# A transformer block on one Trainium2 core: half a column group of the feed-forward input projection moved to the seven-product scheme, and its weight blocks prepared beside the output projection

## The chip, the core and the metric

The kernel runs on one core of a Trainium2 chip. A core has a matrix engine (TensorE, PE in the profile, with PEld for its weight loads), a vector engine (VectorE, DVE), a scalar engine (ScalarE, ACT), a general engine (GpSimd, POOL) and a queue engine (SyncE, SP), which here only issues transfers. Each engine works through its own list of instructions in order and waits at semaphores for the others. Matrix products are accumulated in PSUM, which has eight banks, b0 to b7; everything else lies in SBUF. The metric is the device time of one execution, in microseconds (us).

## What is computed

One decoder block for 512 tokens and a width of 1024. What matters here is its end: the output projection with its residual, the second normalization, and the input projection of a SwiGLU feed-forward network with 2816 hidden columns.

```python
x = x + gate1 * (merged @ w_out)
h2 = rms_norm(x, norm2_g) * (1.0 + scale2) + shift2
f_g, f_u = jnp.split(h2 @ w_ffn_in, 2, axis=-1)
x = x + gate2 * ((jax.nn.silu(f_g) * f_u) @ w_ffn_out)
```

## The kernel before

**Precision.** A product is made of three matmuls (`mm3`, lines 52 to 55): each operand is split into a rounded part `hi` and the rest `lo`, and hi·hi, hi·lo and lo·hi are summed. A weight block therefore costs one ACT copy (to `hi`) and one DVE subtraction (to `lo`) before PE can use it.

**Weights.** They come in blocks of 512 KB. For most of the kernel they are a `stream`: `ensure(n)` issues the transfers ahead (line 92, on SP) into a ring of three buffers, tag `raw` (`RAWB = 3`), and prepares the chunks up to n (`prep`, ACT at L110 and DVE at L114). A transfer is issued when the preparation of the chunk that had the buffer before has been done.

**Output projection** (the loop over `half`). Tokens go in two halves of 256. For each half, eight chunks of `w_out` (n_ = 0 to 7) give two column halves: for the second token half, n_ = 0 to 3 make the first column half and n_ = 4 to 7 the second. Each n_ is 12 matmuls of 128x512 into `po`. When a column half is complete, `resid` adds it to x (two DVE operations, L1108 and L1109, and a square on ACT, L1110, for each of two token tiles). When both are there, `row_rstd` (L1113, L1114) and `norm2_x` (L1130 on ACT, L1132 on DVE) give the normalized rows `xn`.

**Transposes** (`norm2_T`). `xn` of one token half is transposed on PE (L1154) by pairs of 128 columns: pair k2 = 0 to 3 has four transposes into one bank and holds kt = 2·k2 and 2·k2 + 1. From there each kt is evacuated three times: ACT writes `hi` (L1161), DVE (or, for every fourth kt, ACT: L1164) writes the full value `h2f` (L1166), and DVE subtracts to get `lo` (L1167). For token half 0 this is done behind n_ = 2 of token half 1 of the output projection, with pairs 0 to 3 in banks 4 to 7; for token half 1 within group 0, below.

**Group 0 of the feed-forward input** (`pf`). The 2816 gate columns and the 2816 up columns are worked off in groups of 256. Group 0 is done directly: four chunks `WF[0]` to `WF[3]` (gate kh = 0 and 1, up kh = 0 and 1, where kh is the half of the 1024 inputs), each 24 matmuls of 128x256 for each token half. Order: token half 0 with gate kh 0, gate kh 1, up kh 0, then the transposes of token half 1, up kh 1; then token half 1 with all four. `EV` evacuates the sums (L1225 on ACT, L1231 on DVE).

**The direct half of group 1** (`pb`). The gate columns of group 1 are done directly too, with two more stream chunks.

**Seven products.** From the up columns of group 1 on (q = -1 to 17; q even is the gate half, q odd the up half of group 2 + q // 2) a block of 1024 inputs x 256 columns times 512 tokens is cut into 2 x 2 halves on both sides and done with seven half-size products instead of eight (a Winograd form of Strassen's scheme). On the token side the differences of `h2f` are made once (`t_diff`, L1242 to L1245) and split into `TB[1]` to `TB[4]` (`t_split`, L307 and L308). On the weight side `s_issue(q)` fetches two blocks, `ra` (kh 0) and `rb` (kh 1), and `s_prep(q)` gives four pairs of steps, an ACT part a and a DVE part d:

- a0 and d0: `hi` of A11, then on DVE A21 + A22 (L1295, the first that reads both blocks), `lo` of A11 (L1296) and a difference (L1297);
- a1 and d1: `hi` and `lo` of rb (L1301, L1304), then rb less that difference (L1305);
- a2 and d2: `hi` and `lo` of ra (L1309, L1312); a3 and d3: of the new rb (L1316, L1319).

The steps of block q + 1 are laid between the products of block q, so on ACT and DVE they stand in one line with what the products themselves need: copies of sums (`R`, L1537 and L1550; `ps`, L1544 and L1557), which PE waits for before it adds to the bank further on, silu or multiplication at the end (L1527, L1533, L1525, L1531) and two sums (L1562, L1565). One block has 84 matmuls of 128x256, twelve for each product, in the order A, C (S1), C (S2), B (A12), D (S3), D (S4), B (A22).

The order of every engine's list is the order of the program text; nothing is rescheduled.

Of the kernel before, what the change touches and what calls it, by code (L numbers as in the profile page):

```python
# [9 lines left out]
F32 = mybir.dt.float32  # L10
# [7 lines left out]
D = 1024  # L18
# [10 lines left out]
def block_kernel(ctx: ExitStack, tc: tile.TileContext, x, positions, w_ada, b_ada, w_in,  # L29
# [230 lines left out]
    for n_, (h, k0) in enumerate(((0, 0), (1, 0), (0, 2), (1, 2), (0, 4), (0, 6), (1, 4), (1, 6))):  # L260
        W_O.append((h, add_w(w_o, [k0, k0 + 1], 512 * h, 512, V, (None, None, None, "E2", "E0", "E1", "E3", "E4")[n_])))
    mg = mod_sec(5)
    W_F = []
    for g in range(2):
        wh = ["E5", "E6", "E0", "E1"] if g == 0 else None
        W_F.append([group(w_ffn_in, 256 * g, where=wh)])
        if g == 0:
            W_F[0].append(group(w_ffn_in, DFF, where=wh))
    st["limit"] = len(stream)

    KZ, KC = (list(range(12, 16)), list(range(16, 20))), list(range(12)) + [20, 21]
# [859 lines left out]
            else:  # L1131
                V.tensor_scalar(xn[tk], xt[tk], r2[:, tk:tk + 1], None, op0=OP.mult)  # L1132

    def norm2_T(half, kts):
        if half == 0:
            for kh in range(2):
                t = ffn[0].tile([128, 4, 256], F32, name="h2f", tag=f"F{kh}", bufs=1)
                for j in range(4):
                    h2f[kh * 4 + j, 0] = t[:, j]
                h2f["t", kh, 0] = [t[:, 0:2], t[:, 2:4]]  # L1140
        else:
            for kh in range(2):
                h2f["t", kh, 1] = []
                for q in range(2):
                    t = base.tile([128, 2, 256], F32, name="h2f", tag=f"S1_{kh * 2 + q}", bufs=1)
                    h2f["t", kh, 1].append(t)
                    for j in range(2):
                        h2f[kh * 4 + q * 2 + j, 1] = t[:, j]
        for k2 in kts:
            p = bank(4 + k2, "x2T")  # L1150
            for k in range(2):
                kt = k2 * 2 + k
                for e in range(2):
                    T.transpose(p[:, k * 256 + e * 128:k * 256 + (e + 1) * 128],  # L1154
                                xn[2 * half + e][:, kt * 128:(kt + 1) * 128], ident)
            for k in range(2):
                kt = k2 * 2 + k
                g, s = Gc[:, 1, kt:kt + 1], Gc[:, 1, 8 + kt:9 + kt]
                src = p[:, k * 256:(k + 1) * 256]
                hi, lo = (t[:, kt % 4] for t in HB[kt // 4, half])  # L1160
                A.activation(hi, src, AF.Identity, scale=g, bias=s)  # L1161
                hf = h2f[kt, half]
                if kt % 4 == 3:
                    A.activation(hf, src, AF.Identity, scale=g, bias=s)  # L1164
                else:
                    V.tensor_scalar(hf, src, g, s, op0=OP.mult, op1=OP.add)  # L1166
                V.tensor_sub(lo, hf, f(hi))  # L1167

    wch = {}
    WF0 = W_F[0][0] + W_F[0][1]  # L1170
# [76 lines left out]
    def t_split(n):  # L1247
# [7 lines left out]
    NQ = 18  # L1255
    sraw, sw = {}, {}

    def s_issue(q):
        if q >= NQ:
            return  # L1260
        c0 = (2 + q // 2) * 256 + (DFF if q % 2 else 0)
        sraw[q] = []
        for kh in range(2):
            if q % 2 and kh:
                t = ffn[0].tile([128, 4, 2, 128], F32, name="raw", tag="F0", bufs=1)
            else:
                t = base.tile([128, 4, 2, 128], F32, name="raw", tag="raw", bufs=RAWB)
            SY.dma_start(t.rearrange("p j a n -> p j (a n)"),
                         w_ffn_in[kh * 512:(kh + 1) * 512, c0:c0 + 256].rearrange("(j p) n -> p j n", p=128))
            sraw[q].append(t)  # L1270

    def s_pair(q, n):
        if q % 2 == 0:
            return (base.tile([128, 4, 2, 128], F32R, name="hi", tag="hi", bufs=3),
                    base.tile([128, 4, 2, 128], F32R, name="lo", tag="lo", bufs=3))
        if n < 2:
            t = ffn[0].tile([128, 2, 4, 2, 128], F32R, name="sx", tag=f"E{n}", bufs=1)
            return t[:, 0], t[:, 1]
        return tuple(base.tile([128, 4, 2, 128], F32R, name="sx", tag=f"S2_{2 + e}", bufs=1) for e in range(2))

    def s_prep(q):

        if q >= NQ:
            return z_first()
        ra, rb = sraw[q]
        d = sw[q] = {}
        A11, A21, A12, A22 = ra[:, :, 0], ra[:, :, 1], rb[:, :, 0], rb[:, :, 1]

        def a0():
            d["A"] = tuple(base.tile([128, 4, 128], F32R, name="sa", tag=f"S1_{4 + 2 * (q % 2) + e}", bufs=1)  # L1290
                           for e in range(2))
            A.activation(d["A"][0], A11, AF.Copy)

        def d0():
            V.tensor_add(A21, A21, A22)  # L1295
            V.tensor_sub(d["A"][1], A11, f(d["A"][0]))  # L1296
            V.tensor_sub(A11, A21, A11)  # L1297

        def a1():
            d["B"] = s_pair(q, 0)  # L1300
            A.activation(d["B"][0], rb, AF.Copy)  # L1301

        def d1():
            V.tensor_sub(d["B"][1], rb, f(d["B"][0]))  # L1304
            V.tensor_sub(rb, rb, A11[:, :, None, :].to_broadcast([128, 4, 2, 128]))  # L1305

        def a2():
            d["C"] = s_pair(q, 1)
            A.activation(d["C"][0], ra, AF.Copy)  # L1309

        def d2():
            V.tensor_sub(d["C"][1], ra, f(d["C"][0]))  # L1312

        def a3():
            d["D"] = s_pair(q, 2)
            A.activation(d["D"][0], rb, AF.Copy)  # L1316

        def d3():
            V.tensor_sub(d["D"][1], rb, f(d["D"][0]))  # L1319
        return [(a0, d0), (a1, d1), (a2, d2), (a3, d3)]  # L1320


    mgl = list(mg)
# [129 lines left out]
    for half in range(2):  # L1453
        o = slice(half * 256, (half + 1) * 256)
        for w in range(2):
            for ci, i in enumerate(W_F[0][w]):
                hi, lo = chunk[i]
                for j, kt in enumerate(stream[i]["kts"]):
                    for m in range(2):
                        cc = slice(m * 128, (m + 1) * 128)  # L1460
                        mm3(pf[w][m][:, o], (hi[:, j, cc], lo[:, j, cc]), tuple(t[:, j] for t in HB[ci, half]),
                            kt + half == 0, kt == 7, skip_group_check=True)
                if half == 0 and w == 1 and ci == 0:
                    norm2_T(1, range(4))
            if half == 0 and w == 1:
                t_diff()
                ensure(W_F[1][0][0])
            if half == 1:
                EV[w](0)(pf[w])
                ensure(W_F[1][0][1])  # L1470
                if w == 0:
                    t_split(1)
                    s_issue(-1)
                else:
                    t_split(2)
    pre = None
    pb = [bank(b, "pf1") for b in (5, 6)]
    for ci, i in enumerate(W_F[1][0]):
        hi, lo = get(i, 1)
        for j in range(4):  # L1480
            for m in range(2):
                cc = slice(m * 128, (m + 1) * 128)
                for th in range(2):
                    mm3(pb[m][:, th * 256:(th + 1) * 256], (hi[:, j, cc], lo[:, j, cc]),
                        tuple(t[:, j] for t in HB[ci, th]), ci + j + th == 0, ci == 1 and j == 3,
                        skip_group_check=True)
        if ci == 0:
            s_issue(0)
            pre = s_prep(-1)
        for a_, d_ in pre[2 * ci:2 * ci + 2]:  # L1490
            a_()
            d_()
            if d_ is pre[2][1]:
                t_split(3)
    f_evac(1)(pb)


    def sprod(o, wb, hb, start):
# [2 lines left out]
            mm3(o, (wh[:, j], wl[:, j]), (bh[:, j], bl[:, j]), start and j == 0, j == 3, skip_group_check=True)  # L1501

    left = []
    for q in range(-1, NQ):
        g, u = 2 + q // 2, q % 2
        d = sw[q]
        s_issue(q + 2)
# [36 lines left out]
        A.activation(ps[0], R[3], AF.Copy)  # L1544
# [242 lines left out]
```

## Time and profile before

| | |
|---|---|
| Time before, median of 3 runs | 840.51 us (840.35 to 841.24) |
| The profiled execution | 839.88 us, of which the span from the first to the last instruction is 838.0 us |
| DVE, ACT, POOL busy | 79%, 48%, 14% of the span |
| Transfers | 109.09 MB, mean 130 GB/s |
| Granted TensorE clock | 0.998 |

A row of the timeline gives the start, the duration, the engine, the line, the operation, "output <- input" by the program's names, the shape and how many were merged; in brackets stands how long the engine had been idle and what ended that. Matmuls are pipelined: what PE can do is read from the distance between starts, which is shorter than the duration of one. The windows give, for each engine, the busy time in a stretch, with the granted clock, the transfer share and GB/s at the end. A transfer's time to landing counts from its issue.

### The profile page before, as it was taken

The page shows a single profiled execution, that of the slowest core. Times are in us where ns is not written, and L with a number is a line of the kernel's source. Part 1 is how long each engine was busy: PE and PEld are TensorE (multiplying, and loading weights), DVE is VectorE, ACT ScalarE, POOL GpSimd, SP SyncE. Part 2 cuts the span into 40 slices and gives each one's busy share as a digit, 9 for nine tenths or more (in the row PEclk, how much of TensorE's full clock was granted, in tenths as well). Part 3 has the DMA queues.
Part 4 walks back from the last instruction along what each step waited for, and adds up shares of the span by engine and source line. Part 5 has one row for each costly group of instructions (what it writes and reads, how often), then busy time and mean ns, then how long its engine had stood idle before and what let it go on. Part 6 is the DMA issues. An engine that isn't in the chain of part 4 may idle for free.

```text
span 838.0 us, 12892 instructions
## 1 busy us (share of the span) xinstructions
PE 825.4 (98%) x5004; PEld 734.8 (88%) x5004; DVE 664.6 (79%) x1152; ACT 399.6 (48%) x696; POOL 118.2 (14%) x105
## 2 busy tenths in 40 slices
PE   7999999999999999999999999999999999999996
PEld 6888889988888888988888899999999999888885
DVE  7978799788899548887776568989998888985635
ACT  6664445332332227665434355655555555663322
POOL 2060022353344411002210000000000000000001
PEclk9999999999999999999999999999999999999999
DMA  9962362432346551037544032445543334142212
GB/s 299 311 190 72 95 200 78 127 90 86 109 145 200 189 163 51 26 102 248 174 142 165 1 126 76 127 153 156 172 149 102 101 101 150 53 149 101 78 51 100
DMA packets 95677, 109.09 MB, mean 130 GB/s; under 512 B 5617, under 2 KB 76273, under 8 KB 95617
## 3 DMA queue, kind: packets, MB, share of 16 engines
q1 hardware_dynamic: 92512, 101.37, 38.8%
q0 software_dynamic: 2384, 6.10, 2.0%
q8 instruction: 39, 0.64, 0.3%
q10 hardware_dynamic: 720, 0.82, 0.3%
q14 instruction: 22, 0.17, 0.1%
HBM read 105.90 MB, written 2.10 MB: 129 GB/s over the span
## 4 chain that ended last, share of the span: by engine, by line
PE 96%; DMA 1%; DVE 1%; issue 0%; SPq 0%; ACT 0%; POOLq 0%; POOL 0%; DVEq 0%
PE pb L53 9%; PE pb L55 9%; PE pb L54 9%; PE R L53 8%; PE R L54 8%; PE R L55 8%; PE pfo L55 4%; PE pfo L53 4%; PE pfo L54 4%; PE pav L54 2%; PE pav L53 2%; PE pav L55 2%; PE po L54 2%; PE pgb L53 2%; PE pgb L54 2%; PE pgb L55 2%
## 5 line engine op out<-in xcount | busy, mean ns | idle before, releaser
L110 ACT ACTIVATE hi<-raw 128x1024 fp32r<-128x1024 f32 (+2 forms) x85 | 87.7, 1035 | 106.2 <-PE pfo L55 35.3
L114 POOL TENSOR_TENSOR lo<-raw,hi 128x1024 fp32r<-128x1024 f32 x33 | 83.0, 2519 | 213.1 <-ACT hi L110 207.4
L114 DVE TENSOR_TENSOR lo<-raw,hi 128x1024 fp32r<-128x1024 f32 (+2 forms) x45 | 55.6, 1242 | 51.2 <-ACT hi L110 51.1
L53 PE MATMUL pb<-h,hi 128*128 128x512 f32 x192 | 76.4, 398 | 0.0
L55 PE MATMUL pb<-h,lo 128*128 128x512 f32 x192 | 75.8, 395 | 0.0
L54 PE MATMUL pb<-hl,hi 128*128 128x512 f32 x192 | 75.7, 395 | 0.0
L55 PE MATMUL pfo<-hi,gs 128*128 128x512 f32 (+1 forms) x126 | 46.4, 369 | 0.0
L54 PE MATMUL pfo<-lo,gs 128*128 128x512 f32 (+1 forms) x126 | 46.4, 368 | 0.0
L53 PE MATMUL pfo<-hi,gs 128*128 128x512 f32 (+1 forms) x126 | 46.4, 368 | 0.0
L53 PE MATMUL R<-tb,sx 128*128 128x256 f32 x160 | 45.3, 283 | 0.0
L54 PE MATMUL R<-tb,sx 128*128 128x256 f32 x160 | 45.1, 282 | 0.0
L55 PE MATMUL R<-tb,sx 128*128 128x256 f32 x160 | 45.0, 281 | 0.0
L55 PEld LDWEIGHTS pb<-h,lo 128*128 128x128 f32 x192 | 36.0, 187 | 8.7
L54 PEld LDWEIGHTS pb<-hl,hi 128*128 128x128 f32 x192 | 36.0, 188 | 8.4
L53 PEld LDWEIGHTS pb<-h,hi 128*128 128x128 f32 x192 | 36.0, 188 | 8.3
L55 PE MATMUL R<-tb,lo 128*128 128x256 f32 x144 | 40.3, 280 | 0.0
L53 PE MATMUL R<-tb,hi 128*128 128x256 f32 x144 | 40.3, 280 | 0.0
L54 PE MATMUL R<-tb,hi 128*128 128x256 f32 x144 | 40.2, 279 | 0.0
L175 DVE SCALAR_TENSOR_TENSOR acc<-mraw,cols,acc 128x512 f32<-128x512 f32 x38 | 32.1, 845 | 8.7 <-DMA mraw<-in_w_ada_dram 7.8
L54 PE MATMUL pav<-lo,h 128*128 128x256 f32 x128 | 35.8, 279 | 0.0
L53 PE MATMUL pav<-hi,h 128*128 128x256 f32 x128 | 35.7, 279 | 0.0
L55 PE MATMUL pav<-hi,hl 128*128 128x256 f32 x128 | 35.7, 279 | 0.0
(382 smaller groups left out, 2657.6 us busy)
## 6 DMA issues: line engine op xcount, KB each, us to landing
raw<-in_w_ffn_in_dram SPq DMA_DIRECT2D x44, 512.0 KB, 4.0
raw<-in_w_in_dram SPq DMA_DIRECT2D x40, 512.0 KB, 3.8
mraw<-in_w_ada_dram SPq DMA_DIRECT2D x22, 512.0 KB, 3.8
raw<-in_w_ffn_out_dram SPq DMA_DIRECT2D x17, 512.0 KB, 3.6
s<-in_w_ada_dram SPq DMA_DIRECT2D x30, 256.0 KB, 5.6
raw<-in_w_ada_dram SPq DMA_DIRECT2D x10, 512.0 KB, 4.4
raw<-in_w_proj_a_dram SPq DMA_DIRECT2D x8, 512.0 KB, 4.6
raw<-in_w_proj_b_dram SPq DMA_DIRECT2D x8, 512.0 KB, 3.4
```

What stands on the lines that cost most here:

```text
L53: T.matmul(o, wh, rh, start=start, stop=False, **kw)
L54: T.matmul(o, wh, rlo, start=False, stop=False, **kw)
L55: T.matmul(o, wlo, rh, start=False, stop=stop, **kw)
L110: A.activation(hi[:, :m], e["raw"][:, :m], AF.Copy)
L114: e["lo"].tensor_sub(lo[:, :m], e["raw"][:, :m], f(hi[:, :m]))
L175: V.scalar_tensor_tensor(o, w, cs[:, j:j + 1], o, op0=OP.mult, op1=OP.add)
```

## The change

The gate half of group 1 becomes block q = -2 of the seven-product scheme, and the two stream chunks that it needed are gone. The functions `s_issue`, `s_pair` and `s_prep` move ahead of the output projection; so that block q = -2 can be prepared early, four more things are placed otherwise:

- `WF[0]` and `WF[1]` are prepared behind n_ = 1 of the second token half, `WF[2]` behind n_ = 3 and `WF[3]` behind n_ = 4; then the transfers of q = -2 are issued. Steps a0, d0 stand behind n_ = 6, a1 behind n_ = 7, d1, a2 and d2 behind the second `norm2_x`, a3 and d3 behind the last evacuation of `norm2_T`.
- The transposes of each token half are made in two parts, pairs 0 and 1 and then pairs 2 and 3, with 12 (token half 0) or 24 (token half 1) matmuls between them, in banks 4 and 7 alone. In token half 1, `h2f` of every odd kt is written by ACT.
- Blocks q = -2 and q = -1 have both raw blocks in the ring of three (before, `rb` of q = -1 was in tag F0).
- `t_split(3)` and `t_split(4)` come right behind `t_split(2)`, before the first product, instead of between products; the order is 1, 2, 3, multiplication of group 0, 4.

```diff
-    W_F = []
-    for g in range(2):
-        wh = ["E5", "E6", "E0", "E1"] if g == 0 else None
-        W_F.append([group(w_ffn_in, 256 * g, where=wh)])
-        if g == 0:
-            W_F[0].append(group(w_ffn_in, DFF, where=wh))
+    wh = ["E5", "E6", "E0", "E1"]
+    W_F = [group(w_ffn_in, c, where=wh) for c in (0, DFF)]
...
-    def norm2_T(half, kts):
-        if half == 0:
+    def norm2_T(half, kts, after=()):
+        if kts[0]:
+            pass
+        elif half == 0:
...
-            p = bank(4 + k2, "x2T")
+            p = bank(7 if k2 % 2 else 4, "x2T")
...
-                if kt % 4 == 3:
+                if kt % 4 == 3 or half and kt % 2:
                     A.activation(hf, src, AF.Identity, scale=g, bias=s)
...
+            if k2 in after:
+                for fn in after[k2]:
+                    fn()
...
     def s_issue(q):
...
-            if q % 2 and kh:
+            if q > 0 and q % 2 and kh:
                 t = ffn[0].tile([128, 4, 2, 128], F32, name="raw", tag="F0", bufs=1)
...
         def a0():
-            d["A"] = tuple(base.tile([128, 4, 128], F32R, name="sa", tag=f"S1_{4 + 2 * (q % 2) + e}", bufs=1)
+            d["A"] = tuple(base.tile([128, 4, 128], F32R, name="sa", tag="acc", bufs=2) if q == -2 else
+                           base.tile([128, 4, 128], F32R, name="sa", tag=f"S1_{4 + 2 * (q % 2) + e}", bufs=1)
...
                     norm2_x(0)
-                if n_ == 2:
-                    norm2_T(0, range(4))
-                if n_ in (3, 4, 5):
-                    ensure(WF0[n_ - 3])
+                    ensure(WF0[1])
+                if n_ in (2, 3):
+                    norm2_T(0, (0, 1) if n_ == 2 else (2, 3))
+                if n_ in (3, 4):
+                    ensure(WF0[n_ - 1])
+                if n_ == 4:
+                    s_issue(-2)
+                if n_ == 6:
+                    pre = s_prep(-2)
+                    for fn in pre[0]:
+                        fn()
+    pre[1][0]()
     for e in range(2, 4):
         row_rstd(e)
     norm2_x(1)
-    ensure(WF0[3])
+    pre[1][1]()
+    for fn in pre[2]:
+        fn()
...
-                if half == 0 and w == 1 and ci == 0:
-                    norm2_T(1, range(4))
+                if half == 0 and w == 1:
+                    norm2_T(1, (2 * ci, 2 * ci + 1), {3: pre[3]})
             if half == 0 and w == 1:
+                s_issue(-1)
                 t_diff()
-                ensure(W_F[1][0][0])
             if half == 1:
-                EV[w](0)(pf[w])
-                ensure(W_F[1][0][1])
                 if w == 0:
-                    t_split(1)
-                    s_issue(-1)
-                else:
-                    t_split(2)
-    pre = None
-    pb = [bank(b, "pf1") for b in (5, 6)]
-    for ci, i in enumerate(W_F[1][0]):
...
-        if ci == 0:
-            s_issue(0)
-            pre = s_prep(-1)
-        for a_, d_ in pre[2 * ci:2 * ci + 2]:
-            a_()
-            d_()
-            if d_ is pre[2][1]:
-                t_split(3)
-    f_evac(1)(pb)
+                    EV[w](0)(pf[w])
+                t_split(w + 1)
+                if w == 1:
+                    t_split(3)
+                    EV[w](0)(pf[w])
+                    t_split(4)
...
-    for q in range(-1, NQ):
+    for q in range(-2, NQ):
...
-        if q < 0:
-            t_split(4)
```

More of the change, by code (lines that the diff above doesn't have):

```diff
@@ L1167, in norm2_T, with s_issue @@
                 V.tensor_sub(lo, hf, f(hi))
+            if k2 in after:
+                for fn in after[k2]:
+                    fn()
+    NQ = 18
+    sraw, sw = {}, {}
+    def s_issue(q):
+        if q >= NQ:
+            return
+        c0 = (2 + q // 2) * 256 + (DFF if q % 2 else 0)
+        sraw[q] = []
+        for kh in range(2):
+            if q > 0 and q % 2 and kh:
+                t = ffn[0].tile([128, 4, 2, 128], F32, name="raw", tag="F0", bufs=1)
+            else:
+                t = base.tile([128, 4, 2, 128], F32, name="raw", tag="raw", bufs=RAWB)
+            SY.dma_start(t.rearrange("p j a n -> p j (a n)"),
+                         w_ffn_in[kh * 512:(kh + 1) * 512, c0:c0 + 256].rearrange("(j p) n -> p j n", p=128))
+            sraw[q].append(t)
@@ L1169, in block_kernel @@
     wch = {}
-    WF0 = W_F[0][0] + W_F[0][1]
+    WF0 = W_F[0] + W_F[1]
     OORD = (W_O, [W_O[n_] for n_ in (0, 2, 4, 5, 1, 3, 6, 7)])
@@ L1252, in t_split @@
         TB[n] = (t[:, 0], t[:, 1])
[L1255 to L1263, printed above, removed]
-            if q % 2 and kh:
-                t = ffn[0].tile([128, 4, 2, 128], F32, name="raw", tag="F0", bufs=1)
-            else:
[L1267 to L1289, printed above, removed]
-            d["A"] = tuple(base.tile([128, 4, 128], F32R, name="sa", tag=f"S1_{4 + 2 * (q % 2) + e}", bufs=1)
[L1291 to L1320, printed above, removed]
@@ L1455, in block_kernel @@
         for w in range(2):
-            for ci, i in enumerate(W_F[0][w]):
+            for ci, i in enumerate(W_F[w]):
                 hi, lo = chunk[i]
```

47 lines of the change are left out of this document (38 added, 9 removed).

## The prediction

> **What bounds the kernel now.** I read the shares of busy time, then the chain of work that ended last, then the busy time by stage around the change.
>
> ```profile
> span 838.0 us, 12892 instructions
> PE 825.4 (98%) x5004; PEld 734.8 (88%) x5004; DVE 664.6 (79%) x1152; ACT 399.6 (48%) x696; POOL 118.2 (14%) x105
> PE 96%; DMA 1%; DVE 1%; issue 0%; SPq 0%; ACT 0%; POOLq 0%; POOL 0%; DVEq 0%
> ...
> core 0: us, PE busy (x) PEld busy (x) DVE busy (x) ACT busy (x) POOL busy (x), PEclk, DMA share, GB/s
> 487.25:511.85 24.60, 24.60 (x210) 24.59 (x209) 19.13 (x33) 15.55 (x27) 2.07 (x3) 1.00 0.34 108
> 511.85:523.51 11.66, 11.66 (x98) 11.54 (x97) 10.23 (x14) 4.09 (x6) 0.00 (x0) 1.00 0.42 135
> 523.51:533.66 10.15, 10.15 (x87) 10.06 (x85) 10.08 (x13) 7.53 (x14) 0.00 (x0) 1.00 0.33 107
> 533.66:543.70 10.04, 10.04 (x87) 10.04 (x86) 9.31 (x15) 4.75 (x8) 0.00 (x0) 1.00 0.40 125
> ```
>
> TensorE (PE) is the chain, and in these stages it never waits. The four stretches are: group 0; group 1's gate half done directly; block q=-1 by seven products; block q=0. The second number after each stretch is PE busy, then come PEld, DVE and ACT. DVE is the one to watch: 10.08 of 10.15 us in q=-1. An edit here pays only by shortening PE's list, and any new wait of PE costs in full.
>
> **What is removed.** The direct half has 2·4·2·2·3 = 96 matmuls of 128x256; seven products have 7·4·3 = 84.
>
> ```profile
> 487.25 0.28 PE L53 MATMUL pf<-h,wx 128*128 128x256 f32 x1
> ...
> 495.82 1.91 PE L1154 MATMUL x2T<-cst,xn 128*128 128x128 f32 x16
> 497.49 0.36 PE L53 MATMUL pf<-h,wx 128*128 128x256 f32 x1
> ```
>
> Between the first two rows lie 72 such matmuls: 8.57/72 = 0.119 us each, so 12 are worth 1.43 us. By stages it is 11.66 - 10.04 = **1.62 us**, which also counts small gaps at the old block's start; I take 1.62, with 1.43 as the lower bound. Two weight preparations (ACT L110, DVE L114) go as well; they lie off PE's path. This gain alone is 0.19% of 840.51, and about 0.2% is what a measurement of this kernel can tell from no change.
>
> **a. The first transposes in two parts.** The 16 transposes were one run; now eight stand behind quarter n_=2 and eight behind n_=3, and the second eight reuse the banks 4 and 7 of the first.
>
> ```profile
> 471.53 1.91 PE L1154 MATMUL x2T<-cst,xn 128*128 128x128 f32 x16
> 473.19 0.48 PE L53 MATMUL po<-wx,mh 128*128 128x512 f32 x1
> 476.08 0.40 PE L53 MATMUL po<-hi,mh 128*128 128x512 f32 x1
> ...
> 475.90 0.56 ACT L1164 ACTIVATE h2f<-x2T,Gc 128x256 f32<-128x256 f32 x1
> ```
>
> Sixteen take 473.19 - 471.53 = 1.66, eight 0.83. Quarter n_=3 (2.89) then ends at 475.25, k2=2's four transposes at 475.67, and k2=3 must wait until ACT has read kt=3 out of bank 7: 475.90 + 0.56 = 476.46, 476.52 with 0.06 for the signal. PE starts n_=4 at 476.94, not 476.08; with 0.09 more at each restart after transposes (first matmul 0.36 against 0.28 us) PE is **0.95 us** late.
>
> **b. The new weight block in the third raw buffer.** ACT and DVE now do the residual of the first column half before they evacuate k2=2 and 3.
>
> ```profile
> 476.49 0.42 DVE L1167 TENSOR_TENSOR h<-h2f,h 128x256 fp32r<-128x256 f32 x1 [0.63 <-ACT h2f L1164]
> 481.01 0.69 DVE L1108 TENSOR_TENSOR rt<-po,gate1b 128x512 f32<-128x512 f32 x1
> ...
> 476.35 0.56 ACT L1161 ACTIVATE h<-x2T,Gc 128x256 fp32r<-128x256 f32 x1
> 480.08 0.56 ACT L1164 ACTIVATE h2f<-x2T,Gc 128x256 f32<-128x256 f32 x1
> 484.47 2.00 ACT L110 ACTIVATE wx<-raw 128x1024 fp32r<-128x1024 f32 x2
> ...
> 486.80 1.50 SPq L92 DMA_DIRECT2D raw<-in_w_ffn_in_dram  x2
> ...
> raw<-in_w_ffn_in_dram SPq DMA_DIRECT2D x1, 512.0 KB, 3.5
> ...
> DMA to landing us min/median/max: 3.4/3.8/6.0
> ...
> 487.82 1.22 DVE L114 TENSOR_TENSOR wx<-raw,wx 128x1024 fp32r<-128x1024 f32 x1
> 488.96 0.68 DVE L1108 TENSOR_TENSOR rt<-po,gate1b 128x512 f32<-128x512 f32 x1
> 490.29 0.68 DVE L1108 TENSOR_TENSOR rt<-po,gate1b 128x512 f32<-128x512 f32 x1
> ...
> 493.81 1.15 ACT L1130 ACTIVATE xn<-xr,sm 128x1024 f32<-128x1024 f32 x1 [1.29 <-POOL sm L1114]
> ```
>
> The residual starts right behind kt=3's lo, 476.49 + 0.34 = 476.83, 4.18 earlier than before; its squares free ACT at 484.47 - 4.18 = 480.29. From kt=4's hi to kt=7's h2f ACT takes 480.08 - 476.35 = 3.73, so that h2f starts at 484.02 and weight chunk WF[2] 0.46 later, at 484.48: as before. So its buffer comes free as before and SP issues at 486.80. But what it now issues is q=-2's second half, rb, which lands 3.5 us later, at 490.3. DVE is through with WF[3]'s lo at 487.9 (485.55 + 2·1.14 + 0.08; two such subtractions start 488.96 - 487.82 = 1.14 apart), and next in its line is step d0 of q=-2, which reads rb. **Queued behind it are the residual of the last column half, row_rstd and xn.**
>
> ```profile
> 518.20 0.69 DVE L1295 TENSOR_TENSOR raw<-raw 128x512 f32<-128x512 f32 x1 [1.35 <-DMA raw<-in_w_ffn_in_dram]
> 520.14 1.22 DVE L1304 TENSOR_TENSOR sx<-raw,sx 128x1024 fp32r<-128x1024 f32 x1
> 521.39 1.23 DVE L1305 TENSOR_TENSOR raw<-raw 128x1024 f32<-128x1024 f32 x1
> ```
>
> Step d0 takes 520.14 - 518.20 = 1.94. So 490.4 + 1.94 = 492.34 for the residual instead of 488.96: +3.38. ACT's xn moves to 497.19 and ends at 498.34. PE begins pf at 487.25 + 0.95 = 488.20 and is at its transposes 8.57 later, 496.77; first it waits 0.13 for the bank that the second L1108 (490.29 + 3.38) still reads; then, from 496.90, for xn until 498.40, less the 0.10 of one transpose. PE waits **1.53 us** and ends the eight at 499.13. The landing row bounds this: 3.4 to 6.0, so -0.1 to +2.5 us; I take 3.5, the same issue at the same moment.
>
> **c. The second transposes.** Behind xn stands the rest of q=-2's preparation. ACT does a2 (1.06) until 499.30 and kt=0's hi after it. DVE, done with its own xn at 496.74 and with a1 on hand at 496.87, does d1's two operations (521.39 - 520.14 = 1.25 to the second), waits for a2, does d2 from 499.34, and 1.14 later, at 500.48, begins kt=0's h2f.
>
> ```profile
> 497.08 0.54 DVE L1166 TENSOR_SCALAR h2f<-x2T,Gc 128x256 f32<-128x256 f32 x1
> ...
> 500.21 0.56 ACT L1164 ACTIVATE h2f<-x2T,Gc 128x256 f32<-128x256 f32 x1
> ```
>
> From there to the end of kt=3's h2f took 500.21 + 0.56 - 497.08 = 3.69: 504.17. In this half every odd kt now has its h2f on ACT; that shifts 0.54 us from DVE to 0.56 on ACT, and as hi and h2f of a bank follow each other in turn anyway, I leave the pace as it is. PE has k2=2's transposes done at 499.13 + 2.94 + 0.05 + 0.42 = 502.54 and stands before k2=3 until 504.22: **1.73 us** with the 0.05. Half 1 starts at 504.73 instead of 500.43 (511.85 less 96·0.119): 4.30 late. Block q=-2 starts at 504.73 + 11.42 = 516.15.
>
> **d. and e. DVE stays behind.**
>
> ```profile
> 505.33 0.68 DVE L1242 TENSOR_TENSOR h2f<-h2f 128x512 f32<-128x512 f32 x1
> ...
> 510.89 2.35 DVE L114 TENSOR_TENSOR lo<-raw,hi 128x1024 fp32r<-128x1024 f32 x2
> 513.16 1.29 DVE L308 TENSOR_TENSOR tb<-h2f,tb 128x512 fp32r<-128x512 f32 x2
> 514.36 0.68 DVE L1231 TENSOR_TENSOR gq<-fs,pf 128x512 f32<-128x512 f32 x1
> ...
> 526.59 0.38 ACT L1544 ACTIVATE ps<-R 128x256 f32<-128x256 f32 x1 [1.01 <-PE R L55]
> ```
>
> kt=4 to 7 take 4.18 more (475.90 to 480.08), then a3 on ACT and its lo on DVE at 509.35; t_diff from 510.49 for 510.89 - 505.33 = 5.56; four t_splits and the gq pair at 514.36 - 513.16 = 1.20 each: DVE reaches d0 of q=-1 at 522.05, its last part ends at 524.07. ACT's a2 of q=-1 waits for that (to 525.17), and behind a2 on ACT stand q=-2's silu and its ps copy (some 0.3 apart, 0.38 long), to 525.73. PE's seventh product waits for ps: it is ready at 516.15 + 6·1.43 = 524.73, so **1.05 us**. In q=-1 DVE goes on from 523.99: 1.25 and 1.14 to d2 at 526.38, then d3 behind ACT's a3 (526.5 to 527.6) at 527.6, and 1.14 later the two sums of q=-2, to 529.5. Behind these on ACT come two silus, a0 of q=0 and the copy of R0 (0.4, 0.6 and 0.35: 530.75), for which PE's third product, ready at 527.24 + 2.86 = 530.1, waits **0.7**; less the 0.11 that this block lost before (10.15 - 10.04), 0.6.
>
> **Sum.** 0.95 + 1.53 + 1.73 + 0.09 (restart) - 1.62 + 1.05 + 0.6 = **+4.3 us**. The profiled execution is 839.88, so 844.2; the runs' median 840.51 is 0.63 above it: **844.8 us**.
>
> Costed at nothing: rb of q=-1, now in a raw buffer, is released by d2 at 500.5 and wanted at 522. rb of q=0 is released by d2 of q=-1 at 527.6, lands at 531.1, its d2 ends at 536.8 and PE wants it at 539.4; uncovered it would cost its delay less 2.6. The number of transfers is unchanged; POOL keeps its order.
>
> **The clock.** The new pauses could cost more than their length.
>
> ```profile
> 830.00:834.00 4.00, 1.08 (x10) 0.88 (x8) 2.64 (x8) 2.02 (x6) 0.66 (x1) 1.00 0.35 131
> 834.00:838.00 4.00, 0.00 (x0) 0.00 (x0) 0.07 (x1) 0.13 (x1) 0.00 (x0) 0.50 0.35 131
> ```
>
> About 3 us without matmuls go by at clock 1.00 before it falls to 0.50. My longest stretch without column matmuls is 504.73 - 502.07 = 2.7 us. [...]
>
> **Rivals.**
> 1. *DVE's idle time takes it all in; no wait.* DVE idles 24.60 - 19.13 + 11.66 - 10.23 = 6.9 us there, and the new block adds 1.94 + 1.25 + 1.2 + 1.14·2 = 6.7 less two L114 (2.4). Then only -1.62 is left: 838.9 us, no change or just faster. It decides if rb is in place at 487.9 and the evacuations keep ahead of PE; against it, the issue at 486.80. 8%.
> 2. *rb lands before DVE asks.* Then b is 0, c 0.75, the rest stands: +1.8, 842.3. It needs an issue 2.4 us earlier. 10%.
> 3. *The clock halves in c*, for as long as the pause: 2.7 us at half speed, +1.3, so 846.1. 7%.
> 4. *The landing is slow* (6.0 instead of 3.5): +2.5, 847.3. 8%.
>
> My forecast has 60%, with 843.3 to 846 as its own range (0.1 us of error in each of some ten hand-overs); 7% are left for smaller sums between 1 and 2. Range 841.3 to 847: left out are rival 1 and most of rival 4. Slower by over 0.2% (above 842.19): the forecast, 3, 4 and most of 2, 0.84. Within: most of 1, and what is left, 0.13. Faster: 0.03, as the whole gain is below 0.2%.
>
> **What would show it.** a: PE idle about 0.8 us within the first transposes, ended by ACT's h2f. b: DVE idle about 2.5 us before d0's first addition, ended by the raw transfer, and PE idle about 1.4 in the second transposes, ended by ACT's xn. c: about 1.7 more, by ACT's h2f. d, e: PE idle about 1 and 0.7 us, by ACT's ps and R copies. q=0 would start near 538.0 instead of 533.66. Wrong, if PE stays full from 471 to 538 or if DVE does not wait for rb.

## The result, and the profile after

| | before | after |
|---|---|---|
| Median of 6 runs | 840.43 us (840.02 to 841.24) | 844.96 us (844.78 to 845.55) |
| Ratio, 95% interval | | 1.0054 [1.0041, 1.0067] |
| Profiled execution, its span | 839.88, 838.0 us | 845.55, 843.4 us |

The changed kernel is slower by 4.5 us, and the interval lies clear of 1. The page after, its span, the shares of busy time and the chain of work that ended last:

```profile
span 843.4 us, 12878 instructions
PE 826.0 (98%) x4992; PEld 734.1 (87%) x4992; DVE 668.2 (79%) x1157; ACT 403.7 (48%) x706; POOL 118.3 (14%) x105
PE 36%; DVE 4%; ACT 2%; issue 1%; DMA 0%; POOLq 0%; POOL 0%; DVEq 0%; ACTq 0%
```

There are twelve matmuls fewer, and the chain, followed back from the end, no longer runs through PE alone: it stood at PE 96%, with DVE and ACT at 1 and 0%, and now passes through DVE and ACT at 4 and 2%. (The named shares do not add up to the span here, so only the appearance of DVE and ACT is read from this line.) PE's busy share rounds to 98% in both and shows nothing: the stops below come to 6 us in all, 0.7% of the span.

Traces are compared by a distance within each trace, from PE's first matmul of the output projection to the first of block q=0. This leaves out that the profiled run of after started its output projection 1.09 us later. Before:

```profile
440.99 0.39 PE L53 MATMUL po<-hi,mh 128*128 128x512 f32 x1
533.66 0.28 PE L53 MATMUL R<-h,sa 128*128 128x256 f32 x1
```

After:

```profile
442.08 0.39 PE L53 MATMUL po<-hi,mh 128*128 128x512 f32 x1
539.03 0.28 PE L53 MATMUL R<-h,sa 128*128 128x256 f32 x1
```

That is 92.67 us before and 96.95 after: **+4.28 us**, all but 0.25 of the difference of the medians.

The lines have other numbers in the kernel after: L1104 and L1105 are the two additions of the residual, L1126 is ACT's xn, L1152 the transposes, L1159 and L1162 ACT's hi and h2f behind them, L1164 DVE's h2f, L1212 to L1214 step d0, and L1529, L1540 and L1547 the copies of R0, of R1 and the second `ps`. The timeline of PE after, its seven longest stops in this stretch (the brackets give the idle time and what ended it, where the profile saw any; times are 1.09 later than on the scale of before):

```profile
477.60 0.66 PE L1152 MATMUL x2T<-cst,xn 128*128 128x128 f32 x4 [0.71 <-ACT h2f L1162]
495.44 0.39 PE L53 MATMUL pf<-h,wx 128*128 128x256 f32 x1
499.42 0.98 PE L1152 MATMUL x2T<-cst,xn 128*128 128x128 f32 x7 [1.10 <-ACT xn L1126]
505.23 0.66 PE L1152 MATMUL x2T<-cst,xn 128*128 128x128 f32 x4 [1.43 <-ACT h2f L1162]
520.04 0.39 PE L53 MATMUL R<-tb,hi 128*128 128x256 f32 x1
526.75 0.39 PE L53 MATMUL R<-tb,hi 128*128 128x256 f32 x1 [0.75 <-ACT ps L1547]
531.81 0.39 PE L53 MATMUL R<-tb,sx 128*128 128x256 f32 x1 [0.52 <-ACT R L1529]
```

Before had no wait of PE between 471 and 535. What a stop costs is read from the starts of the matmuls around it. By starts the seven are 0.89, 0.22, 1.28, 1.67, 0.28, 1.01 and 0.78 us, 0.18 to 0.26 more than the bracket for the five that have one, since the end of a matmul is modelled. On DVE, the row that stands behind three of them, and the two behind it:

```profile
491.43 0.69 DVE L1212 TENSOR_TENSOR raw<-raw 128x512 f32<-128x512 f32 x1 [2.45 <-DMA raw<-in_w_ffn_in_dram]
493.37 0.68 DVE L1104 TENSOR_TENSOR rt<-po,gate1b 128x512 f32<-128x512 f32 x1
501.49 0.54 DVE L1164 TENSOR_SCALAR h2f<-x2T,Gc 128x256 f32<-128x256 f32 x1
```

The first addition of d0 waits 2.45 us for the transfer of rb, and the residual of the last column half (L1104) queues behind it: at 492.28 on the scale of before, where it stood at 488.96. The busy time by stage after, for group 0, block q=-2 and block q=-1, with the granted clock as the third number from the end:

```profile
488.34:517.08 28.74, 26.20 (x214) 25.28 (x212) 21.76 (x36) 15.97 (x28) 2.07 (x3) 1.00 0.30 92
517.08:528.26 11.18, 10.41 (x86) 10.01 (x85) 11.11 (x17) 6.99 (x14) 0.00 (x0) 1.00 0.00 0
528.26:539.03 10.77, 10.25 (x87) 10.05 (x85) 8.88 (x12) 6.80 (x13) 0.00 (x0) 1.00 0.51 150
```

DVE is busy for 11.11 of the 11.18 us of q=-2: it has no idle time left there. In group 0 it has 7 us of idle time, but 2.45 of them are the wait for rb, with the residual queued behind it.

### The profile page after: what moved, and what is told of

Same layout as the page of the kernel before. It is cut to its first block, busy times and chain, and to the rows that moved or that the text cites. A ratio compares the mean times of both kernels' runs of the same rounds, so it can differ in the third digit from the quotient of the medians.

```text
span 843.4 us, 12878 instructions
## 1 busy us (share of the span) xinstructions
PE 826.0 (98%) x4992; PEld 734.1 (87%) x4992; DVE 668.2 (79%) x1157; ACT 403.7 (48%) x706; POOL 118.3 (14%) x105
## 5 line engine op out<-in xcount | busy, mean ns | idle before, releaser
L110 ACT ACTIVATE hi<-raw 128x1024 fp32r<-128x1024 f32 (+2 forms) x83 | 85.6, 1035 | 107.2 <-PE pfo L55 35.4
L114 DVE TENSOR_TENSOR lo<-raw,hi 128x1024 fp32r<-128x1024 f32 (+2 forms) x43 | 53.3, 1243 | 50.8 <-ACT hi L110 50.7
L53 PE MATMUL R<-tb,hi 128*128 128x256 f32 x160 | 45.1, 282 | 0.8 <-ACT ps L1547 0.7
L55 PE MATMUL R<-tb,lo 128*128 128x256 f32 x160 | 44.9, 280 | 0.0
L54 PE MATMUL R<-tb,hi 128*128 128x256 f32 x160 | 44.7, 279 | 0.0
```

The source lines that it names most:

```text
L53: T.matmul(o, wh, rh, start=start, stop=False, **kw)
L54: T.matmul(o, wh, rlo, start=False, stop=False, **kw)
L55: T.matmul(o, wlo, rh, start=False, stop=stop, **kw)
L110: A.activation(hi[:, :m], e["raw"][:, :m], AF.Copy)
L114: e["lo"].tensor_sub(lo[:, :m], e["raw"][:, :m], f(hi[:, :m]))
```

## The experiments

All times are medians in us, and the kernel before was run again with each set (840.43 for after, 840.19 for e1 to e4, 840.00 for e5 to e8, 840.13 for the rest). What one run gains on another is therefore taken from their differences to their own before. "Stretch" is the distance defined above, less the 92.67 of before. Line numbers in the rows of an experiment are up to a dozen higher where its edits stand further up.

| | time | ratio, 95% interval | stretch |
|---|---|---|---|
| after | 844.96 | 1.0054 [1.0041, 1.0067] | +4.28 |
| e1 four banks | 844.74 | 1.0052 [1.0040, 1.0065] | +4.35 |
| e2 d0 behind | 842.24 | 1.0022 [1.0013, 1.0031] | +1.90 |
| e3 order on ACT | 844.32 | 1.0048 [1.0035, 1.0060] | +3.82 |
| e4 e1 + e2 + e3 | 841.25 | 1.0013 [1.0004, 1.0022] | +0.53 |
| e5 e1, banks cleared | 844.65 | 1.0055 [1.0041, 1.0068] | +4.41 |
| e6 rb in its own buffer | 842.26 | 1.0025 [1.0016, 1.0035] | +1.89 |
| e7 e4, cleared, more order | 840.35 | 1.0003 [0.9994, 1.0011] | +0.04 |
| e8 e7, four steps on POOL | 840.33 | 1.0004 [0.9995, 1.0013] | +0.40 |
| e9 e7 with two banks | 840.91 | 1.0009 [1.0000, 1.0018] | +0.65 |
| e10 e9, h2f on ACT | 839.20 | 0.9991 [0.9982, 1.0000] | -0.73 |
| e12 e10, four banks cleared | 838.48 | 0.9983 [0.9974, 0.9992] | -1.54 |

The question was not whether the predicted stops are there, but whether they are separate costs. The theory of one line says that DVE's list, from the landing of rb on, sets when PE may go on, and that PE meets this line wherever it gets there first. Its rival says that each stop costs by itself.

**e1, transposes in four banks again.** In e1 and e4 part of the sums is left out: the output has a relative error of 0.343. That this is the copied part of R1 and R2 in q=-2, and of one sum of the final products in banks 5 and 6, is the author's reading of the code and was not shown (more of this in the last section). The same instructions run.

```diff
-            p = bank(7 if k2 % 2 else 4, "x2T")
+            p = bank(4 + k2, "x2T")
```

> The transposes again get four banks (4 to 7) in place of two; all else as changed. Theory one line (DVE's line, from the landing of rb on, sets when PE may go on, and PE meets it wherever it gets first): the pauses a and c (0.9 and 1.7 us, ended by ACT's h2f) vanish, but PE then waits longer for the second residual's bank and for TB2 and the copy of R0, and q=0 starts as late as in the changed kernel: 844.9 us (844.5 to 845.3). Rival, each pause costs by itself: 844.96 - 2.6 = 842.4 us.

Measured 844.74: nothing gained, although the stops a and c of the prediction, 2.6 us, are gone. PE's waits in e1:

```profile
494.46 0.39 PE L53 MATMUL pf<-h,wx 128*128 128x256 f32 x1 [0.64 <-DVE rt L1104]
498.44 0.98 PE L1152 MATMUL x2T<-cst,xn 128*128 128x128 f32 x7 [1.09 <-ACT xn L1126]
519.06 0.38 PE L53 MATMUL R<-tb,hi 128*128 128x256 f32 x1 [0.72 <-ACT R L1529]
525.77 0.39 PE L53 MATMUL R<-tb,hi 128*128 128x256 f32 x1 [0.75 <-ACT ps L1547]
530.83 0.39 PE L53 MATMUL R<-tb,sx 128*128 128x256 f32 x1 [0.53 <-ACT R L1529]
```

PE comes earlier to the residual's banks and waits longer there (0.22 became 1.23 by starts), waits for the same xn, for the lo of kt=5 to 7 (0.88 in all, too short each for a bracket), and for a copy in q=-2 (0.28 became 0.98). These three are 2.6 more than in after, as much as a and c had been. On DVE in e1 nothing has moved:

```profile
490.45 0.69 DVE L1212 TENSOR_TENSOR raw<-raw 128x512 f32<-128x512 f32 x1 [2.51 <-DMA raw<-in_w_ffn_in_dram]
492.39 0.68 DVE L1104 TENSOR_TENSOR rt<-po,gate1b 128x512 f32<-128x512 f32 x1
```

The wait at d0 and the residual 1.94 behind it are those of after. This is the line.

**e2, d0 behind the second `norm2_x`.**

```diff
                     pre = s_prep(-2)
-                    for fn in pre[0]:
-                        fn()
+                    pre[0][0]()
...
     norm2_x(1)
+    pre[0][1]()
     pre[1][1]()
```

> DVE's step d0 of q=-2, the first that reads both raw blocks, stands behind the second norm2_x in place of ahead of the last residual; ACT's a0 and a1 stay. Theory one line: DVE no longer idles 2.5 us before the residual, PE does not wait for xn (b, 1.5 us, gone), DVE reaches kt=0's h2f 2.5 us earlier, so c shrinks to about 0.8 and everything behind is 2.5 us earlier: 842.4 us (842.0 to 842.9). Rival, each pause costs by itself: only b goes, 844.96 - 1.5 = 843.4 us. Rival, DVE's total work is the bound and not the idle stretch: no change, 844.9.

842.24: within the range of the line, and outside of both rivals. The longest waits of PE behind its first matmul in e2, over the whole run (total, number, longest; those at `modS` lie before 51 us and were there before):

```profile
PE x2T L1152 <- ACT h2f L1162: 1.4, 2, 0.7
PE modS L413 <- DVE accw L175: 0.7, 2, 0.5
PE R L53 <- ACT ps L1547: 0.7, 1, 0.7
PE R L53 <- ACT R L1529: 0.5, 1, 0.5
```

The wait for xn is gone, and that at the second transposes halved without being touched.

**e3, order on ACT in the two blocks.** In q=-2 a2 of the next block goes behind the ps copy; in q=-1 the two silus of q=-2 go behind the copy of R0.

```diff
-        pre[2][0]()
-        pre[2][1]()
+        if q > -2:
+            pre[2][0]()
+            pre[2][1]()
...
         A.activation(ps[1], R[2], AF.Copy)
+        if q == -2:
+            pre[2][0]()
+            pre[2][1]()
...
-        out_late(1)
+        if q > -2:
+            out_late(1)
...
-        out_late(0)
+        if q > -2:
+            out_late(0)
+        else:
+            left.extend([lambda fn=out_late: fn(1), lambda fn=out_late: fn(0)])
```

> In block q=-2 alone, ACT's a2 of the next block stands behind the ps copy, and the two last silus of q=-2 behind the first copy of R in q=-1; DVE's order is as changed. Both theories: the pauses d and e (1.05 and 0.7 us) come from the place in ACT's line and go, -1.7: 843.3 us (843.0 to 843.7); DVE's next weights are just in time (1.1 us to spare). Rival, DVE itself is what PE meets there: PE waits for d2 or for TB instead and the time stays at 844.9.

844.32, a miss for both theories and for the rival: stops d and e are gone (1.8 us by starts), and 0.4 came of it (0.46 in the trace). PE in e3:

```profile
533.22 0.39 PE L53 MATMUL R<-tb,sx 128*128 128x256 f32 x1 [0.95 <-ACT R L1540]
```

and ACT there:

```profile
531.84 1.06 ACT L1218 ACTIVATE hi<-raw 128x1024 fp32r<-128x1024 f32 x1 [1.21 <-DMA raw<-in_w_ffn_in_dram]
532.80 0.37 ACT L1540 ACTIVATE R<-R 128x256 f32<-128x256 f32 x1
```

The copy that PE wants stands behind a1 of q=0, which waits for a transfer: the same fault as at d0, one block on. The prediction had costed this transfer at nothing because PE wants rb of q=0 itself only at 539.4; it had not asked what queues behind the step that waits for it.

**e4, the three together.**

> All three edits together. Theory one line: PE never waits up to half 1, then meets DVE at kt=7's lo (about 0.6) and at the lo of ra in q=-1 (about 0.8), which leaves the saving of 1.6 nearly used up: 840.4 us (839.6 to 841.2), no change against before. Rival, each pause costs by itself: 844.96 - 1.5 - 2.6 - 1.7 = 839.2 us.

841.25: just above the range of the line, and 2 above its rival. Alone, e1 and e3 gave 0 and 0.4; on top of e2 they are worth 1.0 together (1.4 in the trace), of 3.5 us of stops by starts that e2 still had at the four places they free. What is left in e4 is 0.59 at the lo of kt=6 and 7, 0.97 at the copy of R0 in q=-2, and 0.79 at the copy of e3, which again stands behind a1 and its transfer. So with the first wait lifted the two edits are worth more than before, but not yet their price.

**e5, e1 with a started matmul of 128x256 in banks 5 and 6 ahead of q=-2.** The table calls this cleared. Less of the sums is then left out: the relative error is 0.211 instead of 0.343, in e7 and e8 as well. By the author's reading, which was not shown, the copies of q=-2 then count, and the copied part of the final products is still left out in part.

> The edit of e1_banks (transposes of pairs 0 to 3 in banks 4 to 7 again), and ahead of block q=-2 one started matmul of 128x256 each in banks 5 and 6, so that the copied part of R1 and R2 counts. The before kernel stands at 840.2 in the batch so far, e1_banks at 844.74. Two started matmuls are 2 x 0.119 = 0.24 us of PE. Theory 'one line' (DVE's list from rb's landing on sets when PE may go on): PE has 0.9 us to spare ahead of the seventh product of q=-2, so the 0.24 costs nothing: 844.7 (844.4 to 844.9). Rival 'each pause costs by itself, and PE's own list is the bound between them': 844.74 + 0.24 = 845.0 (844.9 to 845.3).

844.65. 0.24 us more for PE cost nothing that can be seen, as the line has it: the stretch is 0.06 longer than in e1. The interval is too wide to part 844.7 from 845.0 by time alone.

**e6, the landing itself.** No instruction of PE, ACT or DVE is moved; rb gets the buffer of a `w_out` chunk that is done by n_=5, so that it is in place at d0.

```diff
+            if q == -2 and kh:
+                t = ffn[0].tile([128, 2, 4, 2, 128], F32, name="raw", tag="E2", bufs=1)[:, 0]
-            if q > 0 and q % 2 and kh:
+            elif q > 0 and q % 2 and kh:
```

> Second half of the weight block of q=-2 (rb) fetched into a buffer of its own (that of a w_out chunk which is used for the last time at n_=5), so that its transfer is issued some 4 us earlier and has landed when DVE reaches d0. No instruction of DVE, ACT or PE is moved. Theory 'one line, held up by the landing': DVE's 2.45 us of idle time at d0 goes, everything on DVE behind it is 2.45 earlier, PE meets no wait for xn (1.4) and 0.9 less in the second transposes: 844.8 - 2.4 = 842.3 (841.9 to 842.8); the pauses at the first transposes (0.9) and in the two blocks (0.9 and 0.7) stay. Rival 'each pause by itself': only the pause for xn goes, 844.8 - 1.4 = 843.4. Rival 'the work laid ahead of the residual is what costs, not the landing': d0's 1.94 us still stand there, so at most the 0.5 by which the idle time exceeds them goes: 844.3 or more.

842.26. DVE in e6 (its lines are two further down at d0):

```profile
485.47 2.36 DVE L114 TENSOR_TENSOR wx<-raw,wx 128x1024 fp32r<-128x1024 f32 x2 [0.52 <-ACT wx L110]
487.75 0.69 DVE L1214 TENSOR_TENSOR raw<-raw 128x512 f32<-128x512 f32 x1
489.68 0.68 DVE L1104 TENSOR_TENSOR rt<-po,gate1b 128x512 f32<-128x512 f32 x1
```

d0 starts without a wait, at the moment at which DVE is through with WF[3]. The 2.45 us of waiting come back as 2.3 us of time (2.4 in the trace), with d0's own 1.94 us still ahead of the residual. Both rivals, 843.4 and 844.3 or more, are out. So half of the loss is the wait for the landing, not the work that was laid there.

**e7, every place at once:** e2, e3 and e5, and two more moves. In q=-1, a1 and d1 of q=0 go behind the copy that e3 had run into; in q=-2, t_split(4) and a0 go behind the first copy of R0.

> All at once: transposes in four banks with two clearing matmuls (e5), d0 of q=-2 behind the second norm2_x (e2), a2 behind the ps copy and the two silus behind the copy of R0 (e3), and two more: in q=-1 the first steps a1, d1 of q=0, which wait for a transfer, stand behind the copy of R1 into R2, and t_split(4) and a0 of q=-1 stand behind the first copy of R0 in q=-2. If these are all the places where the line of DVE and ACT meets PE: before 840.2 - 1.62 + 0.24 + 0.4 (the short pauses at kt=6 and 7 that e4 had) = 839.2 (838.8 to 839.8). Rival 'DVE has more work in this stretch than PE leaves time for, and the line shows up at the next place as it did in e3': no better than e4, 840.9 or more.

840.35, between the two ranges: in sense the rival was right, since the line shows up again. What is left in e7 on PE, besides 0.6 at the lo of kt=6 and 7:

```profile
524.93 0.39 PE L55 MATMUL R<-tb,sx 128*128 128x256 f32 x1 [0.45 <-DVE sx L1229]
532.31 0.39 PE L53 MATMUL R<-tb,sx 128*128 128x256 f32 x1 [0.22 <-ACT ps L1559]
```

The first stop is DVE's work itself: d2 of q=-1 ends at 524.88, and PE had by then stood 0.45 us for its result. The second is once more the transfer of rb of q=0. DVE and ACT in e7, d2 of q=-1, d0 of q=0, and on ACT a2 of q=0 and the `ps` copy:

```profile
523.66 1.22 DVE L1229 TENSOR_TENSOR sx<-raw,sx 128x1024 fp32r<-128x1024 f32 x1
528.87 0.69 DVE L1212 TENSOR_TENSOR raw<-raw 128x512 f32<-128x512 f32 x1 [2.11 <-DMA raw<-in_w_ffn_in_dram]
530.93 1.06 ACT L1226 ACTIVATE hi<-raw 128x1024 fp32r<-128x1024 f32 x1 [1.00 <-DVE raw L1214]
531.89 0.36 ACT L1559 ACTIVATE ps<-R 128x256 f32<-128x256 f32 x1
```

The transfer is issued when d2 of q=-1 is done, at 524.91, and lands 4.0 us later; d0 waits 2.11 us for it, a2 waits for d0, and the copy that PE wants stands behind a2. So a late DVE is also a late transfer, and that comes back one block on.

**e8, relief for DVE by POOL:** lo of WF[3], d2 and d3 of q=-2 and d3 of q=-1.

```diff
+    stream[W_F[1][1]]["lo"] = P
...
-            V.tensor_sub(d["C"][1], ra, f(d["C"][0]))
+            (P if q == -2 else V).tensor_sub(d["C"][1], ra, f(d["C"][0]))
...
-            V.tensor_sub(d["D"][1], rb, f(d["D"][0]))
+            (P if q < 0 else V).tensor_sub(d["D"][1], rb, f(d["D"][0]))
```

> e7_all_ordered with four subtractions of DVE's list (1.14 us each) put on POOL, which is idle there (2.5 us each on POOL for the same shape in this kernel): lo of WF[3], d2 and d3 of q=-2, d3 of q=-1. If DVE's list is the bound wherever a pause is left, the pauses at kt=6 and 7 go: 0.3 to 0.5 less than e7, 838.8 (838.4 to 839.2). Rival 'POOL is late with them, or slows DVE while it works': not less than e7, 839.2 to 841.

840.33, no gain. POOL in e8:

```profile
486.70 2.50 POOL L114 TENSOR_TENSOR wx<-raw,wx 128x1024 fp32r<-128x1024 f32 x1 [19.54 <-ACT wx L110]
506.74 2.39 POOL L1237 TENSOR_TENSOR lo<-raw,hi 128x1024 fp32r<-128x1024 f32 x1 [6.88 <-PE pf L55]
```

and DVE at the same times:

```profile
486.85 0.68 DVE L1105 TENSOR_TENSOR rt<-po,gate1b 128x512 f32<-128x512 f32 x1
487.57 2.18 DVE L1106 TENSOR_TENSOR xr<-xr,rt 128x512 f32<-128x512 f32 x1
506.74 2.94 DVE L1324 TENSOR_TENSOR h2f<-h2f 128x512 f32<-128x512 f32 x1
```

An operation of 0.69 us takes 2.94 when it meets a POOL operation of 2.39: it is 2.25 longer, nearly the whole of that. These two subtractions, 1.14 each on DVE, are paid back with 1.49 and 2.25. With three of the four moved away from in front of it, DVE begins d2 of q=-1 at 524.24, 0.58 later than in e7.

**e9, e7 with the banks 4 and 7 of the change and no clearing.**

> e7_all_ordered with the transposes back in banks 4 and 7 and without the two clearing matmuls. By the earlier runs the two pauses at the transposes (0.89 and 0.85) come back. Before: 840.0; e7: 840.35. Theory 'one line': in e7 DVE works without a gap from the second transposes to the second product of q=-1, where PE meets it; giving PE a pause further up changes nothing at that place, so 840.35 (840.1 to 840.7). Rival 'each pause by itself': +0.89 +0.85, less 0.24 for the clearing and 0.5 for the short pauses at kt=6 and 7 that need not come then: 841.3.

840.91, between the two, and it decides for neither: two stops of 0.89 and 0.84 come back, less 0.24 for the clearing, 1.49 in all, and the cost against e7 is 0.4 (0.6 in the trace). The shorter stops at kt=6 and 7 and that at 524.93 vanish for it. So more than half of the price is hidden by the line, as its theory says, and the rest is not. The one stop that is left in the two blocks is the second of e7, now 0.74 by starts, with DVE's wait for rb of q=0 ahead of it:

```profile
529.31 0.69 DVE L1212 TENSOR_TENSOR raw<-raw 128x512 f32<-128x512 f32 x1 [2.37 <-DMA raw<-in_w_ffn_in_dram]
532.75 0.39 PE L53 MATMUL R<-tb,sx 128*128 128x256 f32 x1 [0.49 <-ACT ps L1555]
```

**e10, less on DVE's list, by ACT:** e9 with every h2f of token half 1 on ACT.

```diff
-                if kt % 4 == 3 or half and kt % 2:
+                if kt % 4 == 3 or half:
```

> e9 with h2f of the second token half written by ACT for every kt, not only the odd ones: four operations of 0.54 us leave DVE's list, and ACT gets four of 0.56 (starts 0.47 apart). ACT then does hi and h2f of each kt 0.47 apart, 0.94 for a kt instead of 1.05 (2.09 for a pair by the starts on DVE now). Theory 'DVE's line is what PE meets': DVE's line is 8 x 0.1 = 0.8 shorter, the pauses in q=-2 and q=-1 go, and so does half of the one in the second transposes: 840.0 - 1.62 + 0.89 + 0.45 + 0.3 = 840.0 (839.7 to 840.2). Rival 'ACT is as full there as DVE, and the line only changes its engine': 840.35 or more.

839.20, 1.7 less than e9 by one line of text (1.4 in the trace), more than was expected of it: the stop of 0.74 in q=-1 went, and more than half of that in the second transposes (0.84, now 0.31 by starts). Four operations, 2.2 us in all, left DVE's list; d2 of q=-1 begins 0.96 earlier, so rb of q=0 is issued 0.96 earlier. It also landed faster, 3.5 us from its issue where e9 had 4.2; why is not shown, and some of the gain may be that.

**e12, e10 with four banks, and a started matmul over all 512 columns of banks 5 and 6.** Nothing is left out of the sums.

```diff
+    for k in (5, 6):
+        T.matmul(bank(k, "clr"), HB[0, 0][0][:, 0, :128], HB[0, 0][0][:, 0:2].rearrange("p j n -> p (j n)"),
+                 start=True, stop=True, skip_group_check=True)
```

> e10 with the transposes in banks 4 to 7 and a started matmul of the full 512 columns in banks 5 and 6 ahead of q=-2 (2 x 0.234 = 0.47 us). Theory 'DVE's line': both pauses at the transposes go (0.89 and 0.45), 0.47 is added: 840.0 - 0.9 = 839.1 (838.8 to 839.6), below before by about 0.1%. Rival 'PE meets the line again in q=-2 or q=-1': 839.8 to 840.5.

838.48. Against e10 that is 0.72 less: the stops of 0.89 and 0.31, less 2 x 0.234 for the started matmuls. It is beyond the best of the expectation, and **below before by 1.65 us** (0.17%, interval 0.08 to 0.26%). The windows of e12 up to the end of group 0, then q=-2 and q=-1 (the boundary at 522.00 lies 0.28 ahead of the first matmul of q=-1):

```profile
484.00:500.00 16.00, 16.00 (x123) 15.32 (x122) 12.94 (x20) 11.14 (x20) 2.07 (x3) 1.00 0.37 118
500.00:512.36 12.36, 12.36 (x105) 12.28 (x104) 9.23 (x16) 10.21 (x19) 0.00 (x0) 1.00 0.19 62
512.36:522.00 9.64, 9.64 (x83) 9.64 (x82) 9.57 (x15) 5.69 (x11) 0.00 (x0) 1.00 0.00 1
522.00:532.26 10.26, 10.26 (x89) 10.26 (x87) 8.62 (x11) 6.94 (x13) 0.00 (x0) 1.00 0.50 156
```

PE is busy without a break. DVE has 9.57 of 9.64 us in the third window: it is full, and just in time. In the fourth it still waits 1.57 us for rb of q=0, but no copy that PE wants comes late for it. So the saving of the twelve matmuls can be had, but only with the order laid anew and with less on DVE's list than in the change.

## Why the prediction was right, and where its reasoning was not

The forecast of 844.8 us met 844.96. By its own steps (after's times less 1.09):

| step | predicted | measured |
|---|---|---|
| rb of q=-2 issued | 486.80 | 486.79 |
| DVE reaches d0's first addition | 490.4 | 490.34 |
| residual of the last column half | 492.34 | 492.28 |
| first h2f of the second transposes | 500.48 | 500.40 |
| a, first transposes, with the restart | 0.95 | 0.98 |
| b, po bank and xn | 0.13 + 1.40 | 0.22 + 1.28 |
| c, second transposes | 1.73 | 1.67 + 0.06 |
| output projection to q=-2, all of it | +4.30 | +4.14 |
| the two blocks, all of it | +0.03 | +0.14 |
| d, seventh product of q=-2 | 1.05 | 1.01 |
| e, third product of q=-1 | 0.7 | 0.78 |

The two sums are 517.08 - 442.08 = 75.00 against 511.85 - 440.99 = 70.86, and 11.18 + 10.77 = 21.95 against 11.66 + 10.15 = 21.81. What made this possible was to take the instructions of DVE and ACT one by one in the order of their lists, each by the distance of starts in the trace of before, and to ask of each wait what stands behind it.

Two terms were off, in opposite directions. The saving was put at 1.62, and 0.11 more under e, 1.73 in all; without stops the two blocks of e12 take 532.26 - 512.36 = 19.90, so it is 21.81 - 19.90 = 1.91. The difference is a misread boundary: q=0 of before was taken to end at 543.70, but the next block's first matmul stands at 543.60, so that a block takes 9.94 and not 10.04, and 0.10 is missing in each of the two blocks. And a stop in q=-2 ahead of its third product, 0.28 us for a copy that came just too late, was not foreseen. The mechanism was right at each step; that the total came out within 0.2 us is in part luck, since these two and the 0.16 by which the stretch up to q=-2 fell short nearly cancel.

The rivals. Rival 1 failed where the prediction put its condition: rb is not there at 487.9. Rival 2 (rb lands earlier, 842.3) did not happen by itself; e6 made its condition and measured 842.26, with 0.85 left of c where 0.75 was priced. Rival 3: the three windows of after show a clock of 1.00, and so does the longest stretch in which PE had no matmuls but transposes, 2.7 us (502.96 to 505.64), as forecast. In before the last matmul ends at 831.08, and the clock is 1.00 up to 833.50, 0.98 in the mean from there to 834.00, and 0.50 after that: some 2.9 us. No stop in these stages was as long, so what a longer one does to the clock here was not tested. Rival 4: rb was there at 490.34, not 2.5 us later.

What failed was a reading that the sum invites: that each term is the price of its edit. Right as an account of where PE stood, it is wrong as a price list. Steps a and c, 2.68 us by the sum, are worth nothing if undone alone (e1), and d and e, 1.75, are worth 0.4 (e3). The 2.45 us of DVE's wait alone are worth 2.5 or 2.3, undone in either of two ways (e2, e6). A stop of PE ahead of a point at which it must wait for DVE anyway costs little or nothing: nothing in e1, at most half of its length in e9. Where the line no longer meets PE, a stop has its full price again: from e10 to e12 stops of 0.89 and 0.31 go for 0.47 of started matmuls, which is 0.73, and the time falls by 0.72.

And the transfer of rb of q=0, costed at nothing, is a second stop of that kind: covered in after by stop e, laid bare when that was taken away (e3), and still met in e4, e7 and e9. The prediction asked when PE wants that weight block, and not which copies stand on ACT behind the steps that wait for it.

## What to carry to other kernels

Where one engine feeds another in a fixed order, write down the feeder's list with times from the trace of before, find the first entry that waits for a transfer, and look at everything queued behind it: the stops of the fed engine downstream can be largely shadows of that wait. Then look for the same wait in the next block, since its transfer may hang on the same list. Price an edit by undoing it alone and again after the upstream wait is gone; the two answers can be far apart. Before putting work on an idle engine ask whether it stops the busy one: here ACT relieved DVE, and POOL did not.

## What the runs showed of the hardware

DVE and POOL held each other up in e8. DVE's additions and subtractions on SBUF took 2.18 and 2.94 instead of 0.69 us while POOL's of 2.50 and 2.39 ran, and ended 0.55 behind POOL's both times; a POOL operation of that size which began at 495.91, 0.06 us behind a DVE subtraction of 1.22, took 3.42. The DVE operation of 486.85, which has one input in PSUM, kept its 0.68 beside POOL. By what the two hold each other up is not shown.

What a bank had been used for ahead of q=-2 had an effect on the sums in these runs. With transposes in banks 5 and 6 (e1, e4) the output had a relative error of 0.343; with a started matmul over 256 columns of each of the two banks ahead of q=-2 (e5, e7, e8) it had 0.211, and with one over all 512 (e12) nothing is left out of the sums. Nor is anything left out with the transposes in banks 4 and 7 alone (e2, e3, e6, e9, e10), both of which begin q=-2 with a started product. That it is the copied part that was lost, and that e5 lacked it for just the other 256 columns of the final products in banks 5 and 6, which are copied over the full width, is the author's reading of the code; it was not tried by itself, and what in the bank does this is not shown.
